# Four edits to a one-core decoder layer in split fp32: order of the last w_in tiles, width of the weight splits, a second early group behind the second norm, and the last norm's engines

## The chip, the cores and the metric

The kernel runs on one core of one Trainium2 chip. The metric is device time in microseconds (us). The kernel before takes 2956.64 us, the median of three runs (2956.19 to 2958.51). One more execution of it was taken by the hardware profiler; that execution took 2956.17 us, of which the profile's span covers 2954.4 us. The engines are named as in the profile: PE is the matrix engine, PEld its weight load, DVE the vector engine, ACT the activation engine, POOL the GpSimd engine, SP the engine that issues the DMAs.

## The reference

One layer of a decoder is computed for 320 tokens at once: 256 of a prompt and 8 requests of 8 tokens. D_MODEL is 2048 (16 tiles of 128), D_FF is 5632 (44 tiles).

```
x1  = layer_norm(ALPHA*x + 0.5*swiglu_ffn(x, ffn1...), ln1)
q, k, v, o, ig, fg, glu_a, glu_b, gate_a, gate_b = split(x1 @ w_in)
h_a = sigmoid(o) * norm(mlstm(q, k, v, ig, fg, state)) * mh_g       # 4 heads
h_b = silu(layer_norm(depthwise_conv31(glu_a * sigmoid(glu_b)), conv_ln))
mix = (sigmoid(gate_a)*h_a + sigmoid(gate_b)*h_b) @ w_out
x2  = layer_norm(ALPHA*x1 + mix, ln2)
y   = layer_norm(ALPHA*x2 + 0.5*swiglu_ffn(x2, ffn2...), ln3)
```

The states of the four heads (`C`, `n`, `m`) and the last 30 inputs of the convolution are outputs too.

## The kernel before

**Layout and arithmetic.** Activations lie transposed: a tile is 128 features by 320 tokens. Every weight matrix is cut into 128x128 blocks, and all blocks lie in HBM in the order in which they are used (`block_order`). Each fp32 operand is split into a high and a low part, and a block costs three matmuls (`mm3`, L210 to L215): high weights by high x (L213), high weights by low x (L214), low weights by high x (L215). One output tile of 16 blocks is therefore 48 matmuls of 320 columns.

**The weight stream** (`Stream`, L116). Weights come as chunks of 8 blocks (1024 columns, 512 KB). `load` issues a chunk's DMA on SP (L136, four buffers). `_split` takes half a chunk, 512 columns: ACT copies it to `whi` (L148), DVE subtracts to `wlo` (L149). There are five buffers of `whi` and of `wlo`, and splits run three halves ahead of use.

**What sets the order.** `gemm` (L217) walks over k and, inside it, over the accumulators of a group, so a group of four accumulators uses each x tile four times in a row. After every four blocks `tick` (L190) advances each of four lanes of generators by one step; these carry the work beside the matmuls: a head (lane 0), a norm (lane 1), the convolutions of even and odd tiles (lanes 2 and 3). `drain` (L194) runs lanes on until a condition holds. That is the order in which instructions are traced; the library then orders each engine's instructions by a simulated timeline when the program is built (L1200), and each engine works its list from the front. PSUM has five buffers `acc` and three `sm` (L204 to L208). Activation tiles share 72 buffers (`t`).

**The stages.** `ffn(1)`, then `mixer` (w_in), `out_proj` (w_out), `ffn(2)`, `last_norm`. In `ffn` an "up" step makes tiles of w1 and w3 in pairs (the first step two pairs, later ones one), a "down" step one tile of w2 (`ffn_schedule`, L71).

**A norm and what runs over it.** `Norm` gathers sums while tiles come in. The products behind a norm must not wait for it, so `ahead` (L272) makes from each tile a split of z times the gain (`eh`, `el`, with two more columns), and the first group is multiplied with these; `normed` (L283) applies mean and scale to its accumulators afterwards (L287 to L291). Meanwhile `first_group` (L294) makes the true normed tiles `xh`, `xl` in lane 1 (`scaled`: L1134 and L1135; `affine_split`: L500 and L501), which all later groups need. Behind ln1 and ln2 that first group has four accumulators. `states` (L880), which brings the heads' matrix states up to date (`cps`, L914 and L915), starts behind that group in `ffn(2)`.

**The end of w_in.** `w_in_schedule` (L45) lists convolution pairs `a`, `g` with four other tiles behind each pair, and then a tail of 24 tiles: the 16 tiles `gb` of gate_b, then the eight `o` and `ga` tiles of the last head. A `gb` tile needs the convolution's norm: it drains the lanes until its silu tile is done (L980), then multiplies (L981); `mixed` (L936) adds both branches (L939) and splits the sum. An `o` tile needs its head (L986 to L990).

**The last norm** (L459). Of 16 tiles, four are centred by PE (L473, L474), four by POOL and eight by DVE (L467); POOL multiplies its four by the scale, DVE the rest (L486); gain and bias are applied by DVE for every third tile (L491) and by ACT for the others (L493); each tile goes out by a DMA on SP (L494).

Of the kernel before, what the change touches and what calls it, by code (L numbers as in the profile page):

```python
# [9 lines left out]
F32 = mybir.dt.float32  # L10
F32R = mybir.dt.float32r
AF = mybir.ActivationFunctionType
ALU = mybir.AluOpType
# [20 lines left out]
CB = 8  # L34
# [81 lines left out]
class Stream:  # L116


    AHEAD = 3
    RAW_AHEAD = 3  # L120

    def __init__(self, nc, pool, src, n_blocks):
        self.nc, self.pool, self.src = nc, pool, src
        self.n_chunks, self.n_parts = n_blocks // CB, n_blocks // PB
        self.raw, self.parts = {}, {}
        self.next_raw = self.next_split = 0
        self.i = 0
# [9 lines left out]
            yield  # L137
        self.raw[c] = t

    def _split(self, p):  # L140
        nc = self.nc
        c, j = divmod(p, CB // PB)
        raw = self.raw[c][:, j * PB * P:(j + 1) * PB * P]
        if (j + 1) * PB == CB:
            del self.raw[c]
        hi = self.pool.tile([P, PB * P], F32R, tag="whi", name="whi", bufs=5)
        lo = self.pool.tile([P, PB * P], F32R, tag="wlo", name="wlo", bufs=5)
        nc.scalar.activation(hi, raw, AF.Copy)  # L148
        nc.vector.tensor_tensor(out=lo, in0=raw, in1=hi.bitcast(F32), op=ALU.subtract)  # L149
        self.parts[p] = (hi, lo)  # L150

    def advance(self, p):
        while self.next_raw < min(p // (CB // PB) + self.RAW_AHEAD + 1, self.n_chunks):
            for _ in self.load():
                pass
        while self.next_split < min(p + self.AHEAD + 1, self.n_parts):
            self._split(self.next_split)
            self.next_split += 1

    def get(self):  # L160
        p, j = divmod(self.i, PB)
        if j == 0:
            self.parts.pop(p - 1, None)
            self.advance(p)
        self.i += 1
        hi, lo = self.parts[p]
        s = slice(j * P, (j + 1) * P)
        return hi[:, s], lo[:, s]


class Kernel:
# [42 lines left out]
        mm(ps, hi, xl, start=False, stop=False)  # L214
        mm(ps, lo, xh, start=False, stop=last)  # L215

    def gemm(self, accs, xs):  # L217

        n = len(xs)
        for k, (xh, xl) in enumerate(xs):  # L220
# [70 lines left out]
        nc.scalar.activation(t, t, AF.Identity, scale=0.5, bias=w[:, 1:2])  # L291
        return t

    def first_group(self, count, norm, name):  # L294

        accs = [self.acc(T + 2) for _ in range(count)]
# [12 lines left out]
        return [self.normed(ps, norm) for ps in accs], ys  # L309

    def joined(self, x, name):

# [107 lines left out]
    def ffn(self, n, xs, norm=None):  # L420
# [5 lines left out]
        for kind, q, ms in ffn_schedule():  # L426
# [32 lines left out]
    def last_norm(self, norm):  # L459

        nc = self.nc
        by_pe, by_pool = (0, 4, 8, 12), (3, 7, 11, 15)
        z, d = norm.z, {}

        def centre(k):
            eng = nc.gpsimd if k in by_pool else nc.vector
            eng.tensor_tensor(out=z[k], in0=z[k], in1=norm.mean, op=ALU.subtract)  # L467
            d[k] = z[k]

        with self.tc.issue_after(norm.sums.ins):  # L470
            for k in by_pe:
                d[k] = self.acc()
                nc.tensor.matmul(d[k], self.ident, z[k], start=True, stop=False)  # L473
                nc.tensor.matmul(d[k], self.minus_mean, norm.s, start=False, stop=True)  # L474
        for k in (3, 7, 1):
            centre(k)
        with self.tc.issue_after(norm.var.ins):
            for k in (2, 5, 6, 9, 11, 15):
                centre(k)
        first = None  # L480
        for k in list(d) + [k for k in range(KD) if k not in d]:
            with self.tc.issue_after((norm.last if k in d else first).ins):
                if k not in d:
                    centre(k)
                eng = nc.gpsimd if k in by_pool else nc.vector
                mul = eng.tensor_tensor(out=z[k], in0=d[k], in1=norm.r, op=ALU.mult)  # L486
                if eng is nc.vector and first is None:
                    first = mul
                g, b = self.scol("ln3_g", -0.5, k), self.col("ln3_b", k)
                if k % 3 == 1:  # L490
                    nc.vector.tensor_scalar(z[k], z[k], g, b, op0=ALU.mult, op1=ALU.add)  # L491
                else:
                    nc.scalar.activation(z[k], z[k], AF.Identity, scale=g, bias=b)  # L493
                nc.sync.dma_start(out=self.a["yT"][k], in_=z[k])  # L494

    def affine_split(self, u, b):

# [427 lines left out]
    def mixer(self, before):  # L925
# [32 lines left out]
        self.silu_done = 0  # L958
        for n, group in enumerate(w_in_schedule()):
            if ys is None:  # L960
                accs, ys = self.first_group(len(group), before, "ln1")
            else:
                accs = [self.acc() for _ in group]
                self.gemm(accs, ys)
# [255 lines left out]
```

## Time and profile before

| | |
|---|---|
| median of three runs | 2956.64 us |
| the profiled execution, whole | 2956.17 us |
| its span | 2954.4 us |
| PE busy | 2898.7 us (98%) |
| DVE busy | 1894.8 us (64%) |
| ACT busy | 1340.6 us (45%) |
| POOL busy | 70.0 us (2%) |
| instructions | 50389 |

A row of the windows view gives, for a stretch of the span, each engine's busy time with the number of its instructions in brackets, then the mean clock that PE was granted (1.00 is full), the DMA engines' busy share and GB/s. A row of the timeline gives start, length, engine, line, operation, output and inputs, how many like instructions were merged (x3) and, in square brackets, how long the engine had been idle and what ended that. A row of the waits view gives who waited for whom: total us, times, longest. Lengths of neighbouring instructions overlap a little, so the price of one among many is the distance between starts.

### The profile page before, as it was taken

What the parts mean: (1) busy time and instruction counts of PE and PEld (TensorE: products, weight loads), DVE (VectorE), ACT (ScalarE), POOL (GpSimd) and SP (SyncE); (2) the same over time, 40 slices, a digit from 0 to 9 for tenths busy, and PEclk for the clock granted to TensorE, in tenths of its full rate; (3) what the DMA queues carried; (4) which work ended last, traced back from release to release, by engine and by line L of the source; (5) the groups of instructions that cost most, each with busy time, mean ns of one, the idle gap of its engine ahead of it and who ended that gap; (6) DMA issues with size and microseconds to landing.
All of it is one profiled execution on the core that took longest, in us unless ns stands there. A gap on an engine that the chain in (4) does not pass through costs nothing.

```text
span 2954.4 us, 50389 instructions
## 1 busy us (share of the span) xinstructions
PE 2898.7 (98%) x19582; PEld 2868.9 (97%) x19582; DVE 1894.8 (64%) x3495; ACT 1340.6 (45%) x2384; POOL 70.0 (2%) x76
## 2 busy tenths in 40 slices
PE   9999999999999899999999989999999999999997
PEld 9999999999999899999999989998999999999997
DVE  5544444444448999989989885587454455455447
ACT  5433433433445555554554564454433433433444
POOL 0100000000000000000000000201100000000001
PEclk9999999999999999999999999999999999999999
DMA  6444444444444456554645634446455555555542
GB/s 220 150 150 150 150 150 150 150 150 151 150 150 139 125 154 194 153 170 144 202 136 174 194 116 150 150 140 223 150 183 185 198 185 196 201 181 196 176 150 103
DMA packets 171521, 483.22 MB, mean 164 GB/s; under 512 B 51308, under 2 KB 54252, under 8 KB 171280
## 3 DMA queue, kind: packets, MB, share of 16 engines
q1 hardware_dynamic: 171280, 480.00, 49.8%
q8 instruction: 153, 2.51, 0.4%
q14 instruction: 88, 0.72, 0.1%
HBM read 453.04 MB, written 26.89 MB: 162 GB/s over the span
## 4 chain that ended last, share of the span: by engine, by line
PE 96%; DVE 3%; ACT 1%; issue 0%; DMA 0%; DVEq 0%; SPq 0%; ACTq 0%
PE acc L213 31%; PE acc L214 31%; PE acc L215 31%; PE ip L822 1%; DVE z L1135 0%; PE cps L914 0%; DVE wlo L149 0%; PE num L843 0%; DVE cy L1135 0%; DVE z L486 0%; DVE xl L501 0%; PE tv L722 0%; PE sp L690 0%; PE num L214 0%; DVE cy L1134 0%
## 5 line engine op out<-in xcount | busy, mean ns | idle before, releaser
L149 DVE TENSOR_TENSOR wlo<-wraw,whi 128x512 fp32r<-128x512 f32 x1568 | 1084.6, 693 | 879.6 <-ACT whi L148 873.1
L148 ACT ACTIVATE whi<-wraw 128x512 fp32r<-128x512 f32 x1568 | 988.3, 631 | 1441.9 <-PE acc L214 1326.5
L213 PE MATMUL acc<-xh,whi 128*128 128x320 f32 x4480 | 1391.6, 311 | 25.7 <-ACT th L248 15.3
L214 PE MATMUL acc<-xl,whi 128*128 128x320 f32 x4480 | 1388.6, 310 | 6.9 <-DVE xl L501 6.9
L215 PE MATMUL acc<-xh,wlo 128*128 128x320 f32 x4480 | 1386.5, 310 | 2.7 <-DVE wlo L149 2.7
L213 PEld LDWEIGHTS acc<-xh,whi 128*128 128x128 f32 x4480 | 846.8, 189 | 31.0 <-ACT th L248 16.0
L214 PEld LDWEIGHTS acc<-xl,whi 128*128 128x128 f32 x4480 | 846.8, 189 | 13.8 <-DVE xl L501 8.6
L215 PEld LDWEIGHTS acc<-xh,wlo 128*128 128x128 f32 x4480 | 844.6, 189 | 7.1 <-DVE wlo L149 3.2
L213 PE MATMUL acc<-hh,whi 128*128 128x320 f32 x1408 | 434.4, 310 | 0.3 <-ACT whi L148 0.3
L214 PE MATMUL acc<-hl,whi 128*128 128x320 f32 x1408 | 434.0, 309 | 0.0
L215 PE MATMUL acc<-hh,wlo 128*128 128x320 f32 x1408 | 432.9, 309 | 0.0
L214 PEld LDWEIGHTS acc<-hl,whi 128*128 128x128 f32 x1408 | 264.7, 188 | 0.7
L213 PEld LDWEIGHTS acc<-hh,whi 128*128 128x128 f32 x1408 | 264.7, 188 | 0.6 <-ACT whi L148 0.6
L215 PEld LDWEIGHTS acc<-hh,wlo 128*128 128x128 f32 x1408 | 264.2, 188 | 0.0
L622 DVE SCALAR_TENSOR_TENSOR cy<-pu,cw,cy 128x256 f32<-128x256 f32 x480 | 220.9, 480 | 1.2
L448 DVE SCALAR_TENSOR_TENSOR z<-acc,z 128x320 f32<-128x320 f32 x128 | 62.7, 490 | 51.5 <-PE acc L215 49.8
L214 PE MATMUL acc<-ml,whi 128*128 128x320 f32 x256 | 79.2, 310 | 0.0
L213 PE MATMUL acc<-mh,whi 128*128 128x320 f32 x256 | 79.0, 309 | 0.0
L215 PE MATMUL acc<-mh,wlo 128*128 128x320 f32 x256 | 78.7, 309 | 0.0
L438 DVE TENSOR_TENSOR h<-s,acc 128x320 f32<-128x320 f32 x86 | 42.0, 488 | 51.9 <-ACT s L436 51.9
L315 POOL TENSOR_TENSOR z<-xh,xl 128x320 f32<-128x320 f32 x48 | 60.0, 1256 | 621.3 <-DVE h L438 357.1
L436 ACT ACTIVATE s<-acc 128x320 f32<-128x320 f32 x86 | 37.6, 438 | 69.0 <-PE acc L215 69.0
(290 smaller groups left out, 1655.1 us busy)
## 6 DMA issues: line engine op xcount, KB each, us to landing
wraw<-in_wst SPq DMA_DIRECT2D x783, 512.0 KB, 3.3
c<-in_C SPq DMA_DIRECT2D x64, 512.0 KB, 4.4
out_C_s<-c SPq DMA_DIRECT2D x32, 512.0 KB, 3.3
out_yT<-z SPq DMA_DIRECT2D x16, 160.0 KB, 1.9
out_C_p<-cn SPq DMA_DIRECT2D x4, 512.0 KB, 3.0
kv<-vst SPq DMA_DIRECT2D x8, 256.0 KB, 4.9
vst<-kv SPq DMA_DIRECT2D x8, 256.0 KB, 3.2
us<-in_cache SPq DMA_DIRECT2D x16, 120.0 KB, 3.1
```

Source lines behind the costliest of these rows:

```text
L148: nc.scalar.activation(hi, raw, AF.Copy)
L149: nc.vector.tensor_tensor(out=lo, in0=raw, in1=hi.bitcast(F32), op=ALU.subtract)
L213: mm(ps, hi, xh, start=first, stop=False)
L214: mm(ps, hi, xl, start=False, stop=False)
L215: mm(ps, lo, xh, start=False, stop=last)
L315: self.nc.gpsimd.tensor_tensor(out=t, in0=hi.bitcast(F32), in1=lo.bitcast(F32), op=ALU.add)
L436: nc.scalar.activation(s, accs[2 * j], AF.Silu)
L438: nc.vector.tensor_tensor(out=hh, in0=s, in1=accs[2 * j + 1], op=ALU.mult)
L448: nc.vector.scalar_tensor_tensor(out=z[m], in0=ps, scalar=0.5 / ALPHA, in1=z[m], op0=ALU.mult, op1=ALU.add)
L622: nc.vector.scalar_tensor_tensor(out=yp, in0=pu[:, w:w + SEQ], scalar=self.cw[:, i, w:w + 1], in1=yp, op0=ALU.mult, op1=ALU.add)
L822: mm(ip[:32, :], qc[j][:, bs], x, start=j == 0 and n == 0, stop=j == 1 and n == 1)
```

## The change

1. The tail of w_in: the last head's eight `o` and `ga` tiles come ahead of the 16 `gb` tiles.
2. A split covers a whole chunk (1024 columns) in one ACT and one DVE instruction, from the third chunk on; three buffers each in place of five half ones, and two chunks ahead in place of three halves.
3. Behind ln2 a second group, of two accumulators, is multiplied with the `eh`, `el` tiles too; one of the accumulators is an `sm` buffer. `first_group` becomes the generator `first_groups`; early tiles are dropped as the last group walks over them; every third normed tile has an empty step behind it; `states` starts behind the second group.
4. The last norm: nine tiles centred by PE, seven by DVE, all products on DVE, gain and bias on ACT for all; POOL has no part.

```diff
-    tail = [("gb", j) for j in range(KD)] + oga(3)
+    tail = oga(3) + [("gb", j) for j in range(KD)]
...
-    AHEAD = 3
+    AHEAD = 2
     RAW_AHEAD = 3
...
-        hi = self.pool.tile([P, PB * P], F32R, tag="whi", name="whi", bufs=5)
-        lo = self.pool.tile([P, PB * P], F32R, tag="wlo", name="wlo", bufs=5)
-        nc.scalar.activation(hi, raw, AF.Copy)
-        nc.vector.tensor_tensor(out=lo, in0=raw, in1=hi.bitcast(F32), op=ALU.subtract)
-        self.parts[p] = (hi, lo)
...
+        raw = self.raw.pop(c)
+        hi = self.pool.tile([P, CB * P], F32R, tag="whi", name="whi", bufs=3)
+        lo = self.pool.tile([P, CB * P], F32R, tag="wlo", name="wlo", bufs=3)
+        n = PB * P if c < 2 else CB * P
+        for i in range(0, CB * P, n):
+            s = slice(i, i + n)
+            nc.scalar.activation(hi[:, s], raw[:, s], AF.Copy)
+            nc.vector.tensor_tensor(out=lo[:, s], in0=raw[:, s], in1=hi[:, s].bitcast(F32), op=ALU.subtract)
+        self.parts[c] = (hi, lo)
...
-    def gemm(self, accs, xs):
+    def gemm(self, accs, xs, clear=False):
...
+            xh, xl = xs[k]
+            if clear:
+                xs[k] = None
...
-    def first_group(self, count, norm, name):
+    def first_groups(self, norm, name, more=0):
...
+                if more and k % 3 == 2:
+                    yield
+
+        accs = [self.acc(T + 2) for _ in range(4)]
         self.later(tiles(), 1)
-        self.gemm(accs, norm.early)
+        self.gemm(accs, norm.early, not more)
+        if more:
+            yield [self.normed(ps, norm) for ps in accs]
+            del accs
+            accs = [self.acc(T + 2)] + [self.sm([P, T + 2], "acc") for _ in range(more - 1)]
+            self.gemm(accs, norm.early, True)
         self.drain((1,), lambda: len(ys) == KD)
         norm.early.clear()
-        return [self.normed(ps, norm) for ps in accs], ys
+        yield [self.normed(ps, norm) for ps in accs]
+        yield ys
...
+        first = None if xs else self.first_groups(norm, "ln2", 2)
+        for i, (kind, q, ms) in enumerate(ffn_schedule()):
             if kind == "up":
-                if xs is None:
-                    accs, xs = self.first_group(2 * len(ms), norm, "ln2")
-                    self.later(self.states())
+                if first and i < 2:
+                    accs = next(first)
+                    if i == 1:
+                        xs = next(first)
+                        self.later(self.states())
...
-        by_pe, by_pool = (0, 4, 8, 12), (3, 7, 11, 15)
+        by_pe = (0, 1, 2, 4, 6, 8, 10, 12, 14)
+        by_dve = [k for k in range(KD) if k not in by_pe]
...
+        with self.tc.issue_after(norm.var.ins):
+            for k in by_dve[:3]:
+                centre(k)
+        prev = norm.last
+        for k in range(KD):
+            if k in by_pe:
                 d[k] = self.acc()
                 nc.tensor.matmul(d[k], self.ident, z[k], start=True, stop=False)
                 nc.tensor.matmul(d[k], self.minus_mean, norm.s, start=False, stop=True)
...
+            with self.tc.issue_after(prev.ins):
                 if k not in d:
                     centre(k)
...
+                prev = nc.vector.tensor_tensor(out=z[k], in0=d[k], in1=norm.r, op=ALU.mult)
+            nc.scalar.activation(z[k], z[k], AF.Identity, scale=self.scol("ln3_g", -0.5, k), bias=self.col("ln3_b", k))
+            nc.sync.dma_start(out=self.a["yT"][k], in_=z[k])
```

More of the change, by code (lines that the diff above doesn't have):

```diff
@@ L123, in __init__ @@
         self.nc, self.pool, self.src = nc, pool, src
-        self.n_chunks, self.n_parts = n_blocks // CB, n_blocks // PB
+        self.n_chunks = n_blocks // CB
         self.raw, self.parts = {}, {}
@@ L138, in load, with _split, advance @@
         self.raw[c] = t
-    def _split(self, p):
+    def _split(self, c):
         nc = self.nc
[L142 to L145, printed above, removed]
-        hi = self.pool.tile([P, PB * P], F32R, tag="whi", name="whi", bufs=5)
-        lo = self.pool.tile([P, PB * P], F32R, tag="wlo", name="wlo", bufs=5)
-        nc.scalar.activation(hi, raw, AF.Copy)
-        nc.vector.tensor_tensor(out=lo, in0=raw, in1=hi.bitcast(F32), op=ALU.subtract)
-        self.parts[p] = (hi, lo)
-    def advance(self, p):
-        while self.next_raw < min(p // (CB // PB) + self.RAW_AHEAD + 1, self.n_chunks):
+        raw = self.raw.pop(c)
[7 more added lines that the diff above has]
+        self.parts[c] = (hi, lo)
+    def advance(self, c):
+        while self.next_raw < min(c + self.RAW_AHEAD + 1, self.n_chunks):
             for _ in self.load():
                 pass
-        while self.next_split < min(p + self.AHEAD + 1, self.n_parts):
+        while self.next_split < min(c + self.AHEAD + 1, self.n_chunks):
             self._split(self.next_split)
@@ L160, in get @@
     def get(self):
-        p, j = divmod(self.i, PB)
+        c, j = divmod(self.i, CB)
         if j == 0:
-            self.parts.pop(p - 1, None)
-            self.advance(p)
+            self.parts.pop(c - 1, None)
+            self.advance(c)
         self.i += 1
-        hi, lo = self.parts[p]
+        hi, lo = self.parts[c]
         s = slice(j * P, (j + 1) * P)
@@ L215, in mm3 @@
         mm(ps, lo, xh, start=False, stop=last)
-    def gemm(self, accs, xs):
+    def gemm(self, accs, xs, clear=False):
         n = len(xs)
-        for k, (xh, xl) in enumerate(xs):
+        for k in range(n):
+            xh, xl = xs[k]
+            if clear:
+                xs[k] = None
             for ps in accs:
@@ L292, in normed @@
         return t
-    def first_group(self, count, norm, name):
-        accs = [self.acc(T + 2) for _ in range(count)]
+    def first_groups(self, norm, name, more=0):
         ys = []
@@ L425, in ffn @@
         new = Norm(self, z, EPS / ALPHA ** 2, "ln1" if n == 1 else None, KD)
-        for kind, q, ms in ffn_schedule():
+        first = None if xs else self.first_groups(norm, "ln2", 2)
+        for i, (kind, q, ms) in enumerate(ffn_schedule()):
             if kind == "up":
-                if xs is None:
-                    accs, xs = self.first_group(2 * len(ms), norm, "ln2")
-                    self.later(self.states())
+                if first and i < 2:
[3 more added lines that the diff above has]
+                        self.later(self.states())
                 else:
@@ L461, in last_norm @@
         nc = self.nc
-        by_pe, by_pool = (0, 4, 8, 12), (3, 7, 11, 15)
+        by_pe = (0, 1, 2, 4, 6, 8, 10, 12, 14)
+        by_dve = [k for k in range(KD) if k not in by_pe]
         z, d = norm.z, {}
         def centre(k):
-            eng = nc.gpsimd if k in by_pool else nc.vector
-            eng.tensor_tensor(out=z[k], in0=z[k], in1=norm.mean, op=ALU.subtract)
             d[k] = z[k]
-        with self.tc.issue_after(norm.sums.ins):
-            for k in by_pe:
+            return nc.vector.tensor_tensor(out=z[k], in0=z[k], in1=norm.mean, op=ALU.subtract)
+        with self.tc.issue_after(norm.var.ins):
[4 more added lines that the diff above has]
+            if k in by_pe:
                 d[k] = self.acc()
@@ L474, in last_norm @@
                 nc.tensor.matmul(d[k], self.minus_mean, norm.s, start=False, stop=True)
[L475 to L482, printed above, removed]
+            with self.tc.issue_after(prev.ins):
                 if k not in d:
                     centre(k)
[L485 to L494, printed above, removed]
+                prev = nc.vector.tensor_tensor(out=z[k], in0=d[k], in1=norm.r, op=ALU.mult)
+            nc.scalar.activation(z[k], z[k], AF.Identity, scale=self.scol("ln3_g", -0.5, k), bias=self.col("ln3_b", k))
+            nc.sync.dma_start(out=self.a["yT"][k], in_=z[k])
     def affine_split(self, u, b):
@@ L960, in mixer @@
             if ys is None:
-                accs, ys = self.first_group(len(group), before, "ln1")
+                accs, ys = self.first_groups(before, "ln1")
             else:
```

## The prediction

> **What bounds the kernel now.** I read the page first, then the table of windows by stage, then who PE waits for, and then the timelines of the places where it waits.
>
> ```profile
> span 2954.4 us, 50389 instructions
> ...
> PE 2898.7 (98%) x19582; PEld 2868.9 (97%) x19582; DVE 1894.8 (64%) x3495; ACT 1340.6 (45%) x2384; POOL 70.0 (2%) x76
> ...
> PE 96%; DVE 3%; ACT 1%; issue 0%; DMA 0%; DVEq 0%; SPq 0%; ACTq 0%
> ...
> L149 DVE TENSOR_TENSOR wlo<-wraw,whi 128x512 fp32r<-128x512 f32 x1568 | 1084.6, 693 | 879.6 <-ACT whi L148 873.1
> L148 ACT ACTIVATE whi<-wraw 128x512 fp32r<-128x512 f32 x1568 | 988.3, 631 | 1441.9 <-PE acc L214 1326.5
> ```
>
> The chain that ended last is PE for 96%. No edit removes a matmul of the products, so the time can only come from where PE does not run at its pace. The windows show those places (columns: window, length, busy and count of PE, PEld, DVE, ACT, POOL, granted clock, DMA share, GB/s).
>
> ```profile
> 20.00:960.00 940.00, 939.66 (x6407) 939.40 (x6406) 477.87 (x804) 392.49 (x668) 21.07 (x16) 1.00 0.46 152
> 965.00:980.00 15.00, 6.44 (x31) 5.67 (x30) 14.77 (x35) 9.16 (x19) 0.00 (x0) 0.66 0.23 71
> 1050.00:1690.00 640.00, 633.56 (x4283) 616.43 (x4284) 583.72 (x1184) 342.86 (x647) 1.74 (x14) 1.00 0.56 169
> 1690.00:1740.00 50.00, 37.80 (x240) 37.28 (x240) 40.05 (x83) 30.27 (x58) 0.00 (x0) 0.87 0.31 106
> 1740.00:1985.00 245.00, 245.00 (x1673) 245.00 (x1673) 160.79 (x317) 124.09 (x235) 18.07 (x16) 1.00 0.44 149
> 1985.00:2030.00 45.00, 40.60 (x237) 37.18 (x236) 44.34 (x93) 23.76 (x46) 0.00 (x0) 0.92 0.55 181
> ```
>
> The first row gives the price of a product matmul at full pace: 940 / 6407 = 0.147 us. A block is three of them, 0.44 us; a chunk of 8 blocks 3.52 us; an output tile 7.04 us. Against that price 965 to 980 holds 31 x 0.147 = 4.6 us of work in 15 (gap A, behind ln1), 1690 to 1740 holds 240 x 0.147 = 35.2 in 50 (gap B, the tail of w_in), and 1985 to 2030 falls short as well (gap C, behind ln2). From 2932 on the last norm runs with no products left (D).
>
> ```profile
> PE acc L213 <- ACT th L248: 15.3, 3, 10.8
> PE acc L214 <- DVE xl L501: 6.9, 5, 5.7
> ...
> PE acc L215 <- DVE wlo L149: 2.7, 2, 1.4
> ```
>
> Over the whole span PE waits for the weight splits' `wlo` only 2.7 us: the stream is well ahead, and the stalls are the norms'.
>
> **Gap B, the moved tiles.**
>
> ```profile
> 1734.82 0.64 PE L213 MATMUL acc<-xh,whi 128*128 128x320 f32 x1 [10.78 <-ACT th L248]
> ```
> ```profile
> 1732.17 0.47 ACT L263 ACTIVATE mh<-hv 128x320 fp32r<-128x320 f32 x1 [7.60 <-DVE hv L939]
> ...
> 1734.35 0.41 ACT L248 ACTIVATE th<-acc 128x320 f32<-128x320 f32 x1
> ```
> ```profile
> 1709.60 5.31 DVE L1134 TENSOR_TENSOR cy<-cy,mean 128x320 f32<-128x320 f32 x13
> ...
> 1722.05 7.49 DVE L1135 SCALAR_TENSOR_TENSOR cy<-cy,conv_ln_g_scaled,r 128x320 f32<-128x320 f32 x16
> ```
> ```profile
> 1735.00:1740.00 5.00, 5.00 (x19) 5.00 (x20) 3.93 (x8) 3.27 (x9) 0.00 (x0) 0.50 0.00 0
> ```
>
> The first `gb` tiles come off PE while the convolution's norm is still being finished. ACT stands before `mh`, whose input waits for DVE's 16 scalings; the `th` that would empty an accumulator is queued behind it; all five `acc` buffers are full and PE stands for 10.78 us. Then 19 matmuls run at half clock, 5.0 us in place of 19 x 0.147 = 2.8. That is 10.8 + 2.2 = 13.0; the rest of the 50 - 35.2 = 14.8 us is short waits, among them the 1.4 for a `wlo` behind a DVE burst.
>
> In the new order eight tiles that need no convolution norm come first: 8 x 7.04 = 56 us of PE work, and the chain that ends at 1734 now has until about 1780. In ticks (four blocks, 1.76 us each): the last `g` tile is followed by four `o`/`ga` tiles and then eight more, 12 x 4 = 48 ticks, and four more until the first `gb` is finished; the last convolution takes 35 steps, the silu tiles 16, 51 together. So the drain at L980 finds its work done. The head that now comes first has 49 steps and 52 ticks. Nothing in the moved tiles waits on PE's side: `tanh_half` alone frees an accumulator, and four free buffers are 28 us of slack. At w_out's start the last `mix` tile is made by a `gb` where it was made by a `ga`; it is the 16th k of a group of four, 15 x 4 x 0.44 = 26 us into it, and the row 1740 to 1985, with PE busy throughout, shows that this cover holds. I return the 13.0 and leave the 1.8 of short waits, since the bursts of 16 stay. Bounds: 0 (the stall moves with the chain) to 14.8.
>
> **Gap C, the second early group.**
>
> ```profile
> L215 PE MATMUL acc<-eh,wlo x64: 305/310/318, 1976.9 to 2007.1; 128*128 128x322 f32 x64
> ```
> ```profile
> 1994.43 0.49 DVE L243 SCALAR_TENSOR_TENSOR r<-rsq,r 128x320 f32<-128x320 f32 x1
> ...
> 2017.68 1.50 DVE L501 SCALAR_TENSOR_TENSOR xl<-z,par,xh 128x320 fp32r<-128x320 f32 x3
> ```
> ```profile
> 2019.72 0.60 PE L213 MATMUL acc<-xh,whi 128*128 128x320 f32 x1 [1.09 <-DVE late L289]
> ```
> ```profile
> 2015.00:2020.00 5.00, 3.02 (x8) 1.60 (x9) 5.00 (x11) 0.00 (x0) 0.00 (x0) 0.67 0.39 136
> 2020.00:2025.00 5.00, 5.00 (x24) 5.00 (x24) 5.00 (x10) 3.04 (x5) 0.00 (x0) 0.65 0.88 273
> ```
>
> The early group ends at 2007; the normed tiles arrive until 2019; from 2007 on PE takes each `xl` as it comes. Of the 237 records in the 45 us, 12 are `cps` of 512 columns (estimate by width, 512/320 x 0.147 = 0.235 each): 225 x 0.147 + 12 x 0.235 = 35.9, so 9.1 us are lost. The second group adds cover of two tiles, 2 x 7.04 = 14.1 us, to about 2021, when all `xl` are there. What is late next is DVE, busy 44.34 of the 45 us: two more accumulators cost it about 2 us there (products, means, copies), while `states` with its `cps` updates leaves this stretch. PE is then ahead of nothing that it needs until 2021, but the `wlo` behind DVE's bursts remain (one such wait is inside the 9.1). I return 7.5; bounds 0 to 9.1. The added 2 columns on 96 matmuls are under 0.1 us. `sm` has three buffers, and the norm's own sums are done with theirs by then.
>
> One term here hangs on the clock. In 2015 to 2020 PE was never idle for more than about a microsecond at a time, yet ran only 8 matmuls, and the clock fell to 0.67 there; 24 records in the next 5 us at 0.147 make 3.5, so 1.5 us are short. The Trainium skill, TensorE: Matmul & The Clock Gate, Part 1: The HAM clock gate, has the clock halved after a whole idle window of about 3.4 us; by that alone this stretch would not be cold and C would be worth 1.5 us less. I go by the row.
>
> **The weight splits.**
>
> ```profile
> 1047.40 1.06 ACT L598 ACTIVATE parts<-rows 4x1024 fp32r<-4x1024 f32 x1
> ```
> ```profile
> 1049.20 1.22 DVE L599 TENSOR_TENSOR parts<-rows,parts 4x1024 fp32r<-4x1024 f32 x1
> ```
>
> Two other instructions of 1024 columns stand in the trace: 1.06 us on ACT, 1.22 on DVE, against 2 x 0.693 for two halves of `wlo`. DVE sheds some 0.1 us a chunk, but it is not the bound: nothing on the path. The cost is a longer way from a freed buffer to the first use: 1.06 + 1.22 = 2.3 us. A buffer falls free two chunks, 7.04 us, before its next content is due (before: four halves, the same), so 4.7 us of slack are left, and the bursts above (5.31 and 7.49 us) are the only ones seen that exceed it. At the start DMA sets the pace:
>
> ```profile
> 20.69 2.43 ACT L148 ACTIVATE whi<-wraw 128x512 fp32r<-128x512 f32 x4 [2.48 <-DMA wraw<-in_wst]
> ```
>
> ACT waited for a chunk to land at 20.69, and PE used it within a microsecond. A whole chunk is split some 0.4 us (ACT) and 0.5 us (DVE) later than a half: 0 to 1.5 us, taken as +0.6. In the mixer (1050 to 1690, 640 - 633.6 = 6.4 us lost) I take 0, between -4 (a freer DVE) and +6 (blunter queues). Gap A has the same instructions and I take 0, between -3 and +3 for another DVE order.
>
> **D, the last norm.**
>
> ```profile
> 1984.59 3.71 DVE L1134 TENSOR_TENSOR z<-z,mean 128x320 f32<-128x320 f32 x9
> ```
> ```profile
> 2934.47 0.49 DVE L1124 SCALAR_TENSOR_TENSOR v<-pq,v 128x320 f32<-128x320 f32 x1 [1.01 <-PE pq L1120]
> 2934.88 4.71 DVE L467 TENSOR_TENSOR z<-z,mean 128x320 f32<-128x320 f32 x5
> 2939.51 0.48 DVE L242 TENSOR_TENSOR rsq<-rsq,v 128x320 f32<-128x320 f32 x1
> 2940.02 0.49 DVE L243 SCALAR_TENSOR_TENSOR r<-rsq,r 128x320 f32<-128x320 f32 x1
> ...
> 2949.42 0.79 DVE L491 TENSOR_SCALAR z<-z,ln_g_scaled,par 128x320 f32<-128x320 f32 x2
> ```
> ```profile
> 2936.05 0.47 ACT L241 ACTIVATE rsq<-r 128x320 f32<-128x320 f32 x1
> ...
> 2944.84 3.38 ACT L493 ACTIVATE z<-z,par,ln_g_scaled 128x320 f32<-128x320 f32 x6 [0.41 <-DVE z L486]
> ```
> ```profile
> 2934.20 0.70 PE L473 MATMUL acc<-z,cst 128*128 128x320 f32 x2
> 2934.73 0.70 PE L474 MATMUL acc<-ns,minus_mean 128*128 128x320 f32 x2
> ```
>
> The subtraction costs 0.40 us apart with POOL idle (3.71 for nine) and 0.94 with POOL on the same work (4.71 for five). So r, ready for DVE's two steps at 2936.52, came at 2940.51. With three subtractions at 0.40 DVE is free at 2936.2, and r comes at 2936.55 + 1.0 = 2937.55. Then 16 products and 4 subtractions at 0.40 end at 2945.7; PE centres one tile in 1.07 us, nine from 2934.2 to 2943.9, each ahead of its product. ACT's affine costs (3.38 - 0.65) / 5 = 0.546 (0.65 is the last one's length), from 2938.1 on: 15 x 0.546 + 0.65 ends at 2946.9. Before, the last result came at 2950.21. Its DMA, and the end, follow as before: 3.3 us sooner, and up to 4.1 if the last two DMAs no longer queue; taken as 3.7. Bounds: 0 (PE's centring at half clock, 19 us for nine) to 4.5.
>
> **The sum**: -13.0 - 7.5 - 3.7 + 0.6 = -23.6. The profiled execution took 2956.17, 1.8 above its span and 0.5 below the median of the runs; 2956.64 - 23.6 gives **2933 us**.
>
> **The rivals.**
> - *Gap B only shrinks.* ACT's queue holds the accumulators' `th` behind something that waits for DVE's bursts, now between `o` tiles. For it: exactly that happened at 1732. Against: 28 us of buffers against bursts of 7.5. Half of B stays: 2933 + 6.5 = 2940. Chance 0.15.
> - *The second group does not cover C*: DVE, full in that stretch, delays `normed`, so that PE waits for accumulators in place of `xl`; then 2933 + 7.5 = 2940.5. Chance 0.10.
> - *Gap A closes too*, because another order of DVE brings ln1's scale earlier: up to 10 us lie there; 2933 - 9 = 2924. Chance 0.08.
> - *Blunter splits stall the mixer*, the slower end. DVE is busy 583.72 of 640 us there. A chunk that uses up its lead costs the added 2.3 - 0.69 - 0.63 = 1.0 us (the two halves' means from the page); the stretch holds 4283 / 24 = 178 chunks at most. From 24 stalled chunks on the gain is gone; with 40 it is 2933 + 40 = 2973. Against: `wlo` was waited for twice in 2954 us. Chance 0.07, of which 0.04 slower than before by over 0.2% and 0.03 about the same. The Trainium skill, Perfetto Trace Analysis, Optimizing Scalar/DVE Operations, points this way: where these engines are not saturated but cause bubbles elsewhere, smaller instructions deliver sooner. At 64% and 45% they are not saturated, but the bubbles here came from norms, not from splits.
>
> **How the numbers follow.** My forecast has the remaining 0.60. Its own bounds (start, mixer, A, the residues) are about -7 to +8: 2926 to 2941. The first two rivals lie inside that or just above, so 2923 to 2945 leaves out the slower rival and the edges of the others. About 0.2% (6 us) is what a measurement of this kernel can tell from no change. Faster: 0.60 + 0.15 + 0.10 + 0.08 = 0.93.
>
> **What would show it.** The stretch from the last `g` tile to w_out's end has PE at 0.147 us a matmul and clock 1.00, with no wait over 2 us for `th`. Behind ln2, `eh` matmuls count 96 for each of the three lines, and `xh` ones start about 14 us later with no wait for `xl`. `wlo` takes about 1.2 us, 780 or so of them, and PE's total wait for it stays under 5 us. The last result comes about 12.4 us after v starts (2934.47), not 15.7. Gap A is as long as before. I am wrong if a new wait of several microseconds stands at a `gb` or `o` tile, or if PE waits for `whi` or `wlo` dozens of times.

## The result and the profile after

The changed kernel takes 2931.05 us (median of four runs, 2930.7 to 2931.39); the kernel before, run beside it, 2956.41 us (2956.09 to 2958.51). The ratio is 0.9912 with a 95% interval of 0.9899 to 0.9924: 25 us, or 0.9%, faster. The forecast was 2933. The profiled execution took 2931.39 us, 1.8 above its span, as before. The changed kernel was run in one group of runs; the kernel before, run beside each later group, lay between 2955.8 and 2959.09. So a difference of a microsecond or two between kernels of different groups isn't settled by their times, and is read from their traces.

First the page of the changed kernel. Line numbers have moved: the three products of a block are now L217, L218 and L219, the splits L152 and L153.

```profile
span 2929.6 us, 47484 instructions
...
PE 2902.1 (99%) x19602; PEld 2872.1 (98%) x19602; DVE 1788.5 (61%) x2717; ACT 1182.6 (40%) x1609; POOL 49.3 (2%) x68
...
L153 DVE TENSOR_TENSOR wlo<-wraw,whi 128x1024 fp32r<-128x1024 f32 (+1 forms) x786 | 966.9, 1230 | 845.0 <-ACT whi L152 843.9
L152 ACT ACTIVATE whi<-wraw 128x1024 fp32r<-128x1024 f32 (+1 forms) x786 | 830.9, 1057 | 1410.2 <-PE acc L218 1106.1
```

PE does the same products, and 20 matmuls more (five more tiles are centred by PE in the last norm), in a span that is 24.8 us shorter. The wide splits cost 1.23 and 1.06 us, as the rows of 1024 columns in the trace of before had said (1.22 and 1.06). Next the windows that answer to those of before, and PE's waits over the whole span.

```profile
965.00:980.00 15.00, 6.84 (x26) 5.79 (x25) 14.77 (x34) 8.66 (x17) 0.00 (x0) 0.66 0.29 101
1050.00:1690.00 640.00, 637.28 (x4308) 620.00 (x4307) 575.94 (x1033) 319.25 (x500) 1.73 (x14) 1.00 0.56 170
1690.00:1740.00 50.00, 48.97 (x333) 48.71 (x333) 41.63 (x75) 35.12 (x59) 0.00 (x0) 1.00 0.41 136
...
1985.00:2030.00 45.00, 45.00 (x302) 44.55 (x301) 41.00 (x72) 25.35 (x39) 1.05 (x1) 1.00 0.72 240
```
```profile
PE acc L218 <- DVE xl L510: 6.4, 2, 5.9
PE acc L217 <- ACT whi L152: 5.8, 3, 4.5
PE acc L496 <- DVE z L501: 3.8, 1, 3.8
PE acc L217 <- ACT th L255: 2.7, 2, 1.4
PE acc L217 <- ACT xh L509: 1.8, 1, 1.8
```

Gap B (1690 to 1740) has 333 matmuls where it had 240, at clock 1.00 in place of 0.87. Gap C (1985 to 2030) is full. Gap A (965 to 980) stands as it was, and makes the first and the fifth row of the waits. New is the third row, a wait of 3.8 us in the last norm.

Where the 24.8 us went is read from when the same instructions run in both traces: rows of the tile views of `mean` (the heads' sums), `mh` (w_out's input) and `hh` (the input of w2), with first and last start. Before, then after:

```profile
L270 PE MATMUL mean<-xh,one x4: 310/310/315, 1195.5 to 1687.5; 128*128 128x320 f32 x4
L213 PE MATMUL acc<-mh,whi x256: 303/309/316, 1863.7 to 1976.2; 128*128 128x320 f32 x128
L213 PE MATMUL acc<-hh,whi x1408: 302/309/418, 162.3 to 2931.3; 128*128 128x320 f32 x176
```
```profile
L277 PE MATMUL mean<-xh,one x4: 305/308/310, 1192.4 to 1683.9; 128*128 128x320 f32 x4
L217 PE MATMUL acc<-mh,whi x256: 303/308/318, 1847.4 to 1960.0; 128*128 128x320 f32 x128
L217 PE MATMUL acc<-hh,whi x1408: 302/308/314, 162.7 to 2905.5; 128*128 128x320 f32 x176
```

| stretch | shift at its end, us | share of the stretch | forecast |
|---|---|---|---|
| start, to the first `hh` | 162.7 - 162.3 = +0.4 | +0.4 | +0.6 |
| gap A and the mixer, to the last head's `mean` | 1683.9 - 1687.5 = -3.6 | -4.0 | 0 |
| gap B, to the first `mh` | 1847.4 - 1863.7 = -16.3 | -12.7 | -13.0 |
| w_out and gap C, to the last `hh` | 2905.5 - 2931.3 = -25.8 | -9.5 | -7.5 |
| last norm, to the end of the span | 2929.6 - 2954.4 = -24.8 | +1.0 | -3.7 |

So the sum came out near the forecast because two errors cancel: the last norm gave nothing, and the mixer and gap C gave more. The last norm's rows in the changed kernel, PE and then DVE:

```profile
2905.89 2.85 PE L496 MATMUL acc<-z,cst 128*128 128x320 f32 x10
2908.58 0.70 PE L1128 MATMUL ps<-ns,mean_d 128*128 128x320 f32 x2
2909.12 2.85 PE L497 MATMUL acc<-ns,minus_mean 128*128 128x320 f32 x10
2911.81 0.70 PE L1129 MATMUL pq<-sq,mean_d 128*128 128x320 f32 x2
2916.31 1.43 PE L496 MATMUL acc<-z,cst 128*128 128x320 f32 x2 [3.79 <-DVE z L501]
2917.53 1.27 PE L497 MATMUL acc<-ns,minus_mean 128*128 128x320 f32 x2
```
```profile
2906.09 0.49 DVE L467 SCALAR_TENSOR_TENSOR z<-acc,z 128x320 f32<-128x320 f32 x1 [3.25 <-PE acc L219]
...
2912.62 0.49 DVE L1133 SCALAR_TENSOR_TENSOR v<-pq,v 128x320 f32<-128x320 f32 x1 [5.01 <-PE pq L1129]
2913.03 1.28 DVE L487 TENSOR_TENSOR z<-z,mean 128x320 f32<-128x320 f32 x3
```

The norm's own sums are `ps` and `pq`, and everything behind waits for them: `v`, the scale `r`, the products. In the changed kernel five tiles' centring stands before them on PE: ten matmuls ahead of `ps`, ten more ahead of `pq`, 2.69 us each time. `v` starts 6.5 us after the last `z` (2906.09 to 2912.62); before, it was 2.5 (2931.94 to 2934.47).

### The profile page after: what moved, and what is told of

It reads as the page before. It is cut to its first block, busy times and chain, and to the rows that moved or that the text cites. A ratio compares the mean times of both kernels' runs of the same rounds, so it can differ in the third digit from the quotient of the medians.

```text
span 2929.6 us, 47484 instructions
## 1 busy us (share of the span) xinstructions
PE 2902.1 (99%) x19602; PEld 2872.1 (98%) x19602; DVE 1788.5 (61%) x2717; ACT 1182.6 (40%) x1609; POOL 49.3 (2%) x68
## 4 chain that ended last, share of the span: by engine, by line
PE 98%; ACT 1%; DMA 1%; DVE 1%; issue 0%; SPq 0%; ACTq 0%; DVEq 0%
PE acc L219 31%; PE acc L217 31%; PE acc L218 31%; PE ip L831 1%; PE cps L923 1%; DMA xraw<-in_xT 0%; DVE z L1144 0%; PE sp L699 0%; PE num L852 0%; ACT whi L152 0%; PE acc L496 0%; PE acc L497 0%; PE num L219 0%; DMA wraw<-in_wst 0%; PE num L218 0%; PE tv L731 0%
## 5 line engine op out<-in xcount | busy, mean ns | idle before, releaser
L153 DVE TENSOR_TENSOR wlo<-wraw,whi 128x1024 fp32r<-128x1024 f32 (+1 forms) x786 | 966.9, 1230 | 845.0 <-ACT whi L152 843.9
L152 ACT ACTIVATE whi<-wraw 128x1024 fp32r<-128x1024 f32 (+1 forms) x786 | 830.9, 1057 | 1410.2 <-PE acc L218 1106.1
L217 PE MATMUL acc<-xh,whi 128*128 128x320 f32 x4448 | 1377.3, 310 | 11.6 <-ACT whi L152 5.8
L218 PE MATMUL acc<-xl,whi 128*128 128x320 f32 x4448 | 1374.9, 309 | 6.4 <-DVE xl L510 6.4
L219 PE MATMUL acc<-xh,wlo 128*128 128x320 f32 x4448 | 1375.0, 310 | 0.0
L217 PEld LDWEIGHTS acc<-xh,whi 128*128 128x128 f32 x4448 | 838.3, 189 | 16.8 <-ACT whi L152 6.3
L218 PEld LDWEIGHTS acc<-xl,whi 128*128 128x128 f32 x4448 | 838.2, 188 | 12.2 <-DVE xl L510 7.2
L219 PEld LDWEIGHTS acc<-xh,wlo 128*128 128x128 f32 x4448 | 836.0, 188 | 4.7 <-issue 0.7
L218 PE MATMUL acc<-hl,whi 128*128 128x320 f32 x1408 | 434.4, 309 | 0.0
L219 PE MATMUL acc<-hh,wlo 128*128 128x320 f32 x1408 | 433.7, 309 | 0.0
L217 PE MATMUL acc<-hh,whi 128*128 128x320 f32 x1408 | 432.7, 308 | 0.0
L218 PEld LDWEIGHTS acc<-hl,whi 128*128 128x128 f32 x1408 | 264.6, 188 | 0.7
L217 PEld LDWEIGHTS acc<-hh,whi 128*128 128x128 f32 x1408 | 264.2, 188 | 0.0
L219 PEld LDWEIGHTS acc<-hh,wlo 128*128 128x128 f32 x1408 | 264.1, 188 | 0.0
L217 PE MATMUL acc<-mh,whi 128*128 128x320 f32 x256 | 79.0, 309 | 0.0
L218 PE MATMUL acc<-ml,whi 128*128 128x320 f32 x256 | 78.9, 308 | 0.0
L219 PE MATMUL acc<-mh,wlo 128*128 128x320 f32 x256 | 78.9, 309 | 0.0
L924 DVE SCALAR_TENSOR_TENSOR c<-c,wc,cps 128x512 f32<-128x512 f32 x64 | 47.4, 745 | 28.3 <-PE cps L923 28.1
```

Of the source, the lines that this page charges most:

```text
L152: nc.scalar.activation(hi[:, s], raw[:, s], AF.Copy)
L153: nc.vector.tensor_tensor(out=lo[:, s], in0=raw[:, s], in1=hi[:, s].bitcast(F32), op=ALU.subtract)
L217: mm(ps, hi, xh, start=first, stop=False)
L924: nc.vector.scalar_tensor_tensor(out=c0[u][:, j, :], in0=c0[u][:, j, :], scalar=self.wc[:, h, b:b + 1], in1=cp, op0=ALU.mult, op1=ALU.add)
```

## The experiments

The theory: the gains are the three covered waits (B, C and a little in the mixer), and the last norm fails because PE's centring was let ahead of the sums. Each part is undone, or done by itself. All diffs are against the changed kernel.

**The tail in its old order.**

```diff
-    tail = oga(3) + [("gb", j) for j in range(KD)]
+    tail = [("gb", j) for j in range(KD)] + oga(3)
```


> The changed kernel with the tail of w_in in its old order (the 16 gb tiles, then the last head's o and ga tiles). My theory: gap B was a lack of PE work while the convolution's norm is finished, and the eight tiles are that work. The stall for a tanh and the half-clock stretch come back, about 11 + 2 us: 2944 us (2941 to 2946). Rival (the gap went because DVE and ACT became lighter with the wide splits): no change, 2930 to 2933.

Measured: 2947.93 us (2945.52 to 2948.5), ratio to the kernel before 0.9966 (0.9954 to 0.9978): 17 us of the gain are gone, more than the theory gave (13) and outside its range, 2941 to 2946. The window of the tail and PE's wait in it:

```profile
1690.00:1740.00 50.00, 36.55 (x223) 36.02 (x223) 37.12 (x69) 26.45 (x43) 0.00 (x0) 0.83 0.32 106
```
```profile
1722.15 7.48 DVE L1144 SCALAR_TENSOR_TENSOR cy<-cy,conv_ln_g_scaled,r 128x320 f32<-128x320 f32 x16
...
1732.31 0.47 ACT L270 ACTIVATE mh<-hv 128x320 fp32r<-128x320 f32 x1 [7.43 <-DVE hv L948]
...
1734.50 0.41 ACT L255 ACTIVATE th<-acc 128x320 f32<-128x320 f32 x1
...
1734.96 0.63 PE L217 MATMUL acc<-xh,whi 128*128 128x320 f32 x1 [11.39 <-ACT th L255]
```

This is the stall of before, link by link, and it ends at the same moment (1734.96 here, 1734.82 before), though PE had come to the tail 3 us earlier (the last head's `mean` at 1684.5, against 1687.5). A gain ahead of a stall is lost in it when the stall's end is set by DVE and ACT; with the stall gone the mixer's gain counts too. That is the difference between 13 and 17.

**Two tiles ahead, and four.** In the second kernel the last norm has its sums first as well (below), so it is compared with that one's 2926.27 us.

```diff
-    tail = oga(3) + [("gb", j) for j in range(KD)]
+    tail = oga(3)[:2] + [("gb", j) for j in range(KD)] + oga(3)[2:]     # the first
+    tail = oga(3)[:4] + [("gb", j) for j in range(KD)] + oga(3)[4:]     # the second
```


> The changed kernel with only two tiles (one o, one ga) ahead of the gb tiles and the other six behind them. My theory counts cover: two tiles are 14 us of PE work against a stall of 11 us, so little or nothing comes back: 2931 to 2934 us. Rival (what counts is the number of ticks before the first gb, 51 steps against 28 ticks, so that the drain traces the norm's work in one heap ahead of the gb): most of gap B comes back, 2940 to 2944 us.

> The changed kernel with the last norm's sums first (2926.3 us), and only four tiles (o12, ga12, o13, ga13) ahead of the gate tiles in place of eight. With none ahead the tail lost 16.8 us, with two 6.9, that is 5 us a tile. Theory of cover: with four the wait of 3.5 us for th and the half clock behind it are gone: 2926 to 2928 us. Rival: what the tiles ahead bring to ACT and DVE delays the chain as well (with two it ended 3.4 us later), so that about half of the 6.9 stays: 2929 to 2931 us.

Measured: with two 2939.28 us (2938.97 to 2940.36), ratio 0.994 (0.9925 to 0.9955), 8.2 slower than the changed kernel: the cover theory had said that two tiles would do, and this fell. The rival's 2940 to 2944 is near, but not met either. With four 2927.11 us (2926.28 to 2927.97), ratio 0.9894 (0.9879 to 0.9909), within the spread of the one with eight. PE's waits in the tail with two tiles ahead, and the stretch that follows:

```profile
PE acc L217 <- ACT th L255: 3.5, 1, 3.5
PE acc L219 <- DVE wlo L153: 1.4, 1, 1.4
```
```profile
1740.00:1745.00 5.00, 5.00 (x22) 5.00 (x21) 2.82 (x8) 3.50 (x9) 0.00 (x0) 0.55 0.04 14
```

The stall now ends at 1738.4, 3.4 us later than with none ahead, since the tiles ahead bring DVE and ACT their own work and splits: from 1690 to the stall's end DVE has made 13 `wlo` of 1.22 us where it had made 9 with none ahead. Then PE runs for about 6 us at half clock. Cover of 14 us against a wait of 11 leaves 3.5, and the clock costs some 2.5 more. By the first `mh` the kernel is 6.9 behind (1854.3 against 1847.4); the rest of the 8.2 comes after the tail. With four the wait is gone (only 0.71 us, for a `whi`, stands there). The rival counted ticks before the first `gb` tile, 28 against 51 steps; four tiles make them 36, still too few, and the stall is gone, so that count isn't what decides. So cover is the right idea, but its size is not the length of the old stall.

**Splits of 512 columns as before.** The class `Stream` of the kernel before, everything else as changed.

```diff
+        hi = self.pool.tile([P, PB * P], F32R, tag="whi", name="whi", bufs=5)
+        lo = self.pool.tile([P, PB * P], F32R, tag="wlo", name="wlo", bufs=5)
```


> The changed kernel with the old weight stream: 512 columns a split, five buffers, three halves ahead. In the stage of the heads and convolutions the changed kernel lost about 2.7 us of PE time where the kernel before lost 6.4. My reading after the result: the wide splits took some 0.15 us a chunk off DVE and ACT and so shortened those waits; then 3 to 5 us come back, 2934 to 2936 us. The rival from the prediction (blunter splits cost time): 2926 to 2930 us. That the splits' width does nothing: 2930.5 to 2931.5 us.

Measured: 2932.85 us (2932.59 to 2934.09), ratio 0.9918; 1.8 slower than the changed kernel, less than the theory's range of 2934 to 2936. Its mixer, and PE's waits there:

```profile
1050.00:1690.00 640.00, 633.06 (x4279) 615.59 (x4278) 583.48 (x1183) 343.25 (x646) 1.73 (x14) 1.00 0.57 170
```
```profile
PE acc L213 <- ACT th L251: 4.5, 2, 2.8
PE tv L727 <- ACT v L973: 1.3, 1, 1.3
PE pb L679 <- DVE parts L604: 1.1, 1, 1.1
```

These are 4279 matmuls against the changed kernel's 4308 in the same 640 us: 29 x 0.147 = 4.3 us. That is the whole gain of the mixer, so it comes from the wide splits. PE's waits say where: 6.9 us here, as in the kernel before, against 2.7 in the changed kernel, all of it for `th`. The longest, 2.8 us at 1328, ends on a `th` that stands in ACT's list behind two table loads of 1.28 us each; the changed kernel's wait at that place is 1.4. Both ACT and DVE have less to do with the wide splits, ACT 319 us in place of 343 and DVE 576 in place of 583; which of them shortened the waits isn't separated, but most of the waits end on ACT. About half of the gain is given back by w_out (first `mh` at 1849.7 against 1847.4). The Trainium skill, Perfetto Trace Analysis, Optimizing Scalar/DVE Operations, gives two rules, larger operations where the engine is saturated and smaller ones where it is not but causes bubbles; the prediction took the second from the engines' shares of the whole span, 64% and 45%. In this stage DVE is 91% busy with the narrow splits and ACT 54%, and the larger operations gained.

**One early group behind ln2.**

```diff
-                if first and i < 2:
+                if first and i < 1:
                     accs = next(first)
-                    if i == 1:
-                        xs = next(first)
-                        self.later(self.states())
+                    xs = next(first)
+                    self.later(self.states())
...
-        first = None if xs else self.first_groups(norm, "ln2", 2)
+        first = None if xs else self.first_groups(norm, "ln2")
```


> The changed kernel with a single early group of four accumulators behind ln2, and states started behind it, as before. My theory: the second group covers the time until the normed tiles are there; gap C comes back, 9 us by the traces: 2938 to 2941 us. Rival (the gap went because DVE was freed by the wide splits and by other orders): under 4 us come back, 2931 to 2935 us.

Measured: 2938.4 us (2936.7 to 2938.98), ratio 0.9935 (about 7.3 slower than the changed kernel), as the theory said. PE's waits between 1985 and 2035:

```profile
PE acc L218 <- DVE xl L509: 2.5, 3, 1.4
PE acc L217 <- DVE late L296: 1.8, 1, 1.8
```

The waits for `xl` are back, and one for `late` with them. The trace is 8.6 us behind at the last `hh` (2914.1 against 2905.5), and 1.2 shorter behind it, of which more below. In the changed kernel the same view of this stretch is empty.

**The last norm as before, and with its sums first.** The first kernel has the function of the kernel before; the second holds PE's centring behind the norm's sums.

```diff
                 d[k] = self.acc()
-                nc.tensor.matmul(d[k], self.ident, z[k], start=True, stop=False)
-                nc.tensor.matmul(d[k], self.minus_mean, norm.s, start=False, stop=True)
+                with self.tc.issue_after(norm.sums.ins):
+                    nc.tensor.matmul(d[k], self.ident, z[k], start=True, stop=False)
+                    nc.tensor.matmul(d[k], self.minus_mean, norm.s, start=False, stop=True)
```


> The changed kernel with the old last norm (POOL, centring on PE behind the sums). The traces put the stretch from the last product to the end of the span at 22.5 us before and 23.5 after, so my theory after the result is that the new last norm costs 1 us: 2930.0 us (2929.5 to 2930.7). The prediction's step (the new last norm gains 3.7 us): 2934.7 us.

> The changed kernel with PE's centring matmuls of the last norm held behind the matmuls of the two sums, as in the kernel before; nothing else. Theory: ten passes with the identity and ten with the mean's matrix now stand ahead of the sums on PE and hold the variance back by 4 us; behind the sums they cost nothing, since DVE and ACT set the pace from there. The variance comes 2.5 us after the last product in place of 6.5, and the time is 2926 us (2925 to 2927.5). Rival (PE's centring of nine tiles is the bound, at a clock that falls in the pause): the time is 2930 to 2932 us.

Measured: the old last norm 2929.94 us (2929.54 to 2930.78), ratio 0.9908; sums first 2926.27 us (2925.45 to 2927.21), ratio 0.9895 (0.9879 to 0.9912). Both as the theory said: as changed, the new last norm costs about a microsecond here, and with its sums first it gains 3.7 against the old one, which is the prediction's figure. PE, and then ACT's sixteen affines, in the kernel with the sums first:

```profile
2907.11 0.81 PE L1129 MATMUL ps<-ns,mean_d 128*128 128x320 f32 x2 [1.11 <-DVE ns L1053]
2907.75 0.70 PE L1130 MATMUL pq<-sq,mean_d 128*128 128x320 f32 x2
2908.29 0.70 PE L497 MATMUL acc<-z,cst 128*128 128x320 f32 x2
2908.83 0.70 PE L498 MATMUL acc<-ns,minus_mean 128*128 128x320 f32 x2
```
```profile
2912.30 8.83 ACT L503 ACTIVATE z<-z,par,ln_g_scaled 128x320 f32<-128x320 f32 x16 [1.68 <-DVE z L502]
```

That ACT row ends at 2921.13, and `v` starts at 2908.56 in this kernel: 12.6 us, where the prediction had 12.4.

The microsecond isn't a fixed price. From the last `hh` product to the end of the span the changed kernel takes 23.9 us, the old last norm 22.8 (the kernel before) and 22.9; the five other kernels that have the new last norm without its sums first take 22.6 to 22.9. In all six with the new one PE stands for 3.8 us and soon runs its pairs at half pace, but with the old tail, for one, a pair takes 0.70 again 3.3 us after PE goes on, and in the changed kernel only after 6.3 (2916.31 to 2922.61). So this last norm is worth between nothing and a loss of 1 us, as long as the centring stands ahead of the sums.

**A second early group behind ln1 too.** Gap A was left by the change. The first kernel does there what the change does behind ln2; the second adds the sums-first edit.

```diff
-    groups = [[("a", 0), ("g", 0), ("a", 1), ("g", 1)]]
-    steps = range(2, KD)
+    groups = [[("a", 0), ("g", 0), ("a", 1), ("g", 1)], [("a", 2), ("g", 2)]]
+    steps = range(3, KD)
...
-            if ys is None:
-                accs, ys = self.first_groups(before, "ln1")
+            if n < 2:
+                accs = next(first)
+                if n == 1:
+                    ys = next(first)
```


> The changed kernel with a second early group behind ln1 too: the convolution's third pair of tiles as a group of two accumulators multiplied with the early tiles. Gap A, the one that no edit touched, loses about 10 us. If the mechanism of gap C (two tiles of PE work cover the wait for the normed tiles) carries over, 7 to 10 us go: 2921 to 2924 us. Rival (DVE, at 96% there, has the normed tiles and the accumulators' scaling to do before anything else, so the gap moves behind the second group): 2928 to 2933 us.

> The second early group behind ln1 and the sums ahead of the centring together. If both theories hold their gains add: 2916 to 2919 us. If one falls, the time is that of the other alone.

Measured: 2941.71 us (2941.62 to 2942.1), ratio 0.9948, slower than the changed kernel by 10.7; with the sums first 2937.37 us (2936.93 to 2937.92), ratio 0.9933. The first misses its theory and its rival; the second, 4.3 faster than the first, misses what was expected of it too. Two windows and three rows of it:

```profile
930.00:1000.00 70.00, 66.70 (x432) 64.94 (x431) 62.82 (x129) 36.23 (x57) 0.00 (x0) 0.95 0.42 132
1330.00:1690.00 360.00, 350.91 (x2360) 341.95 (x2359) 310.74 (x539) 175.78 (x271) 0.74 (x6) 0.99 0.53 167
```
```profile
1339.27 0.41 PE L277 MATMUL var<-xh,one 128*128 128x320 f32 x1 [1.72 <-ACT xh L270]
...
1342.15 0.64 PE L277 MATMUL var<-xl,one 128*128 128x320 f32 x1 [1.81 <-DVE xl L271]
1348.34 0.63 PE L217 MATMUL acc<-xh,whi 128*128 128x320 f32 x1 [5.56 <-ACT q L980]
```

The first window has gained: 432 matmuls against the changed kernel's 399 in the same stretch, 33 x 0.147 = 4.9 us, as expected of the cover. The second has 2360 against its 2438, 78 fewer or 11.5 us, most of it in one place: around 1340 a head's sums on PE wait for splits that DVE has not reached, and the next product then waits for an accumulator that ACT has not emptied; from 1345 to 1350 the clock is 0.50. Taking a2 and g2 out of the loop had also moved every other tile of w_in (none behind that pair, 4.3 behind each later one), and the product for the heads' gates (`gates_product`) to one tile later. Whether the group or the order was to blame was open, and two more kernels were made, both with the sums first and with the other tiles at their old places: one with a2 and g2 as the second group, one with a2 alone.

```diff
+    groups = [[("a", 0), ("g", 0), ("a", 1), ("g", 1)], [("a", 2), ("g", 2)]]
+    groups = [[("a", 0), ("g", 0), ("a", 1), ("g", 1)], [("a", 2)], [("g", 2)]]     # a2 alone
     steps = range(2, KD)
...
-        groups += [[("a", i)], [("g", i)]]
+        if i > 2:
+            groups += [[("a", i)], [("g", i)]]
...
-            if n == 2:
+            if n == 1:     # the pair
                 self.gates_product(ys)
```


> The changed kernel with the last norm's sums first (2926.3 us) and, as in the two runs before, the pair a2, g2 multiplied as a second early group behind ln1; but the other tiles of w_in keep their old places (four behind every pair, the first four right behind a2, g2), where those two runs had put none behind that pair and 4.3 a step behind the others. Theory: the second group itself closes gap A and gains 4.9 us (33 more matmuls of 0.147 us in 930 to 1000), and the 10 to 15 us lost afterwards came from the shifted order, with heads, convolutions and their drains at other phases: then 2921.5 us (2919 to 2925). Rival: the second group behind ln1 itself loses the time, since DVE, over 90% busy there, starts the mixer's lanes later: then 2930 to 2938 us.

> The same with a second early group of one tile only (a2; g2 comes behind it as a group of its own with the normed tiles), so that the order of all tiles is that of the changed kernel. Theory: one tile is 7.04 us of cover against some 8 us of waits, of which 6 go: 2920.5 us (2919 to 2924). Rival as above: 2930 to 2938 us. If the shift of the lanes by one tile is nothing and DVE's extra work eats the cover: 2926 us.

Measured: the pair 2923.59 us (2922.76 to 2926.3), ratio 0.9884 (0.9869 to 0.9898), as its theory said; a2 alone 2926.63 us (2924.12 to 2927.52), ratio 0.9893 (0.9877 to 0.991). With the old places the same group costs nothing later. The pair's windows:

```profile
930.00:1000.00 70.00, 66.70 (x441) 64.12 (x440) 62.82 (x130) 35.91 (x57) 0.00 (x0) 0.98 0.42 131
1330.00:1690.00 360.00, 360.00 (x2438) 351.40 (x2437) 323.66 (x575) 173.34 (x270) 0.74 (x6) 1.00 0.56 172
```

So the loss of about 14 us against it (2937.37 - 2923.59) came from the order, with the gates' product in it; why just this order brings the three engines together at 1340 was not taken further. The pair is the fastest kernel of the study by its median, 2.7 us ahead of the one with the sums first alone; their intervals overlap, but w_out starts 4.3 us earlier (1843.1 against 1847.4). With a2 alone PE's largest wait is this:

```profile
PE acc L218 <- DVE late L297: 10.7, 1, 10.7
```

Four accumulators of the first group and one of the second are all five buffers, so g2 stands until the first of them has been normed; the pair takes its second accumulator from the other pool, and its wait for `late` is 2.9 us. The time is that of the last case in what was expected (2926), but for this reason, which no case had named.

## Why the prediction was right, and where it was wrong

- **Gap B, 13.0 returned**: right, 12.7 by the times of the same instructions, clock 1.00, one wait of 1.03 us left (for a `whi`). The run with the old order shows the place; its 17 hold the mixer's gain as well. The claim that four free buffers and eight tiles give ample slack held: four tiles are enough, two are not. The rival that B only shrinks describes the kernel with two tiles.
- **Gap C, 7.5 returned**: the mechanism was right and the size somewhat too small. 9.5 by the times up to the last `hh`; one product shortly behind the gap comes at 2114.1 in place of 2139.3, 25.2 sooner, of which 16.3 were there at the first `mh`: 8.9, nearly all of the 9.1 that were lost there. Undoing it costs 7.3 (5.3 to 8.3 with the spread of the runs), 8.1 by the traces between the first `mh` and the last `hh`. What was held back, 1.6, was for DVE in that stretch, said to be full. It is nearly full: in the same stretch of the work, now 16 us sooner (1969 to 2014), it is busy 43.2 of 45 us, with 6 updates of `states` where there were 11. But PE has no wait there at all, and no `wlo` was late. `eh` matmuls are 160 in each line over the span where they were 128, so 96 behind ln2, as said. The rival that DVE takes the place of `xl` fell.
- **The mixer, taken as 0 between -4 and +6**: this term was mis-sized. -4.0 with gap A, and gap A did not move, so it is the mixer's, at the lower bound; the narrow splits show 4.3 us on the spot. The reason for 0 was that DVE sheds little and is not the bound, and the lower bound was for a freer DVE alone. But PE's 6.9 us of waits there end on single instructions of ACT and DVE, 5.8 of them on ACT's `th` and `v`, and these came sooner with the wide splits (2.7 us left). ACT's list was no part of the sum. The slower rival (40 stalled chunks) fell: no row for `wlo` stands among PE's waits.
- **The start, +0.6**: +0.4; but the other traces with the same start have the first `hh` anywhere from 162.2 to 163.3, so the term is neither borne out nor refuted.
- **Gap A, 0**: right, 26 matmuls in the window where there were 31; the rival that it closes too fell, and closing it needed an edit of its own.
- **The last norm, -3.7**: this step failed; it measured +1.0, and about 0 in the five other kernels that have it. The rows for subtraction without POOL were right (three in 1.28 us, 0.40 apart, as said), and so was everything from `v` to the last result, 12.4 forecast and 12.6 measured once the sums come first. What failed is the sentence that PE centres nine tiles "from 2934.2", behind the sums as before: it carried over the order of PE's queue, while the change made five of the nine tiles' centring free to go ahead of `ps` and `pq`, and the library, which orders each engine's list by a simulated timeline, put them there. So `v` came 4.0 us late. A second cost follows: PE then has no free accumulator and is idle for 3.79 us, and a pair of matmuls takes 1.27 us behind that in place of 0.70, until 2922; the last result comes 13.6 us after `v`. The Trainium skill, TensorE: Matmul & The Clock Gate, Part 1: The HAM clock gate, has the clock halved after an idle window of about 3.4 us; the 3.79 us here, with a granted clock of 0.50 from 2916 to 2920, agree with it. In the kernel with the sums first there is no such pause and every pair of the centring takes 0.70.

The total was right partly by luck: 4.7 us too much hope in the last norm against some 6 too little in the mixer and gap C.

## What to carry to other kernels

A matmul without a dependence on the critical sum is a candidate to be put ahead of it; where the order of an engine's queue is made by a scheduler, a step that is "behind" something must be tied behind it, and a forecast must ask what the edit sets free. Cover for a wait is worth the matmuls ahead of it less the work that those matmuls bring to the engines which end the wait, so it needs more than the old wait's length, and the buffers to hold it. A wait in a stage is read at the instruction on which it ends, and at what stands before that in its engine's list; an engine's share of the stage doesn't show it. Insert cover without moving the rest of a tuned order: here the same group gained or lost by the order alone.

## What the runs showed that was not expected

- Over the same products, from the last `mh` to the last `hh`, the traces of kernels with no difference there run from 945.1 to 947.9 us, with no wait over 0.3 us in any: a spread of pace of 0.3%. It repeats: the changed kernel and the two that differ from it in the last norm alone have 945.4 each, the first two with a second group behind ln1 947.9 each. So it is not noise of a single trace but goes with what ran before; what sets it is open. Shares of 1 to 2 us in a table like the one above can hold it.
- The clock fell after a wait of only 2.07 us. In the kernel with the tail in its old order PE waits for a `wlo` at 1712.9; four tenths of a microsecond after it goes on, it falls to half pace until 1719. The columns are those of the windows view, as above.

```profile
1712.00:1715.00 3.00, 0.94 (x7) 0.67 (x5) 3.00 (x7) 1.53 (x3) 0.00 (x0) 1.00 0.00 0
1715.00:1717.00 2.00, 2.00 (x9) 2.00 (x10) 2.00 (x4) 1.96 (x3) 0.00 (x0) 0.60 0.54 127
1717.00:1719.00 2.00, 2.00 (x10) 2.00 (x10) 1.97 (x4) 0.14 (x1) 0.00 (x0) 0.55 0.64 207
1719.00:1721.00 2.00, 2.00 (x16) 2.00 (x15) 0.35 (x1) 1.06 (x1) 0.00 (x0) 1.00 0.83 238
```

  19 matmuls in 4 us where 27 fit at 0.147: 1.2 us beside the 2.07. The waits of 1.42 us (before) and 1.43 us (two tiles ahead) at this place left the clock at 1.00; behind the 2.8 us in the mixer with narrow splits it was 0.81 from 1330 to 1335. So a wait shorter than the Trainium skill's 3.4 us window can do it, which bears out the prediction's choice of the row at gap C.
